# TensorE's matmuls in two stages of a streaming encoder layer: order of tracing released

## The chip, the core and the metric

The kernel runs on one core of a Trainium2 chip. The metric is the device time of one execution in microseconds (us). PE is TensorE's matmul side, PEld its weight loads, DVE VectorE, ACT ScalarE, POOL GpSimd, SP the engine that issues most DMAs. "Granted clock" is the share of full speed that TensorE's clock had: 1.00 is 2.4 GHz, 0.50 is 1.2 GHz.

## The reference

One inference step of one layer: 512 prompt tokens and 32 decode tokens (544 columns in all), width 1024, everything fp32.

```
h = rmsnorm(x); u = h @ w_in            # [q k v | r k v + three low-rank inputs | two gates]
A = differential attention (8 heads, two softmax maps, chunk mask; decode tokens see 512 cached rows)
B = RWKV-7 recurrence (16 heads of 64; per-token state update S = S*w + sa*(kk*a) + v*k, y = S r)
x = x + (sigmoid(g_A) * (A @ w_o_da) + sigmoid(g_B) * (B @ w_o_rw)) @ w_out
x = x + (silu(c1) * c2) @ w_down        # c = causal conv of rmsnorm(x) @ w_up
y = rmsnorm(x)
```

## The kernel before

All activations lie transposed, 128 rows of features by 544 columns of tokens. A large product with a weight matrix ("dense work") goes one block of 128 output rows at a time. `dense_g` takes two PSUM banks from the pool `psd` (3 banks), one for each half of the 544 columns, and runs 48 matmuls of 128x272 over eight slices of the contraction: each weight is split into a high and a low part (`wh`, `wl`), each activation too, and three of the four products are kept. `load_w` fetches a weight tile of four slices by DMA, ACT writes `wh` (L218), DVE or POOL writes `wl` (L219); the pool holds four such pairs, so about 96 matmuls' worth. When the block is done, ACT or DVE takes the result out of the two banks, and only then are they free.

Stage 1 (about 74 to 650 us of the profile) is the recurrence with the dense work of the input projection beside it. It has these strands, each a Python generator:

- `elementwise`: for each of 8 pairs of heads `rw_rates` and `rw_elem`: low-rank products (tiles `lwh`, `lwl`) and sums over a head (`bonesr`), each a group of two matmuls into a bank of the pool `misc` (2 banks), with DVE and ACT work between. They need the projections r, k, v of their pair (tiles `r`, `kr` with two buffers, `vv` with one).
- `recurrence`: for each half of the heads (4 pairs) `rw_super` (products `misc<-arL,bkL`, an inverse computed on DVE with 32x32 transposes at L635, L675, L680, two joining steps) and `rw_chain`: 8 chunks, each a loop of `psq<-S,arL` and `psq<-uv,mt`, a DVE copy `qs`, `psq<-qs,XT`, copies `uv` by DVE and ACT, `psq<-uv,bkt`, the state `S` on DVE, and outputs into `psy`. Each chunk also transposes the next keys and values (`misc<-cst,bkL`, `misc<-cst,vC`), which ACT copies to `bkt` (2 buffers) and `uv` (3 buffers).
- `rw_sample` (decode tokens), `norms` (group norm of the chains' output) and `rotary`.

Stage 2 (about 650 to 913 us) is attention by heads and blocks of 128 queries: `sc<-xK,xQ` scores, softmax on DVE and ACT, `tp<-cst,pd` transposes, `po<-vtok,pdt` weighted values, and per head a normalization whose result `on` (L1122) frees the bank `po`. The dense work that stage 1 left over, and then `w_orw`, run beside it. Stage 3 (from 913 us on) is dense work alone: `w_oda` (reading `dh`, `dl`, which attention writes head by head), `w_out`, `w_up`, `w_down`.

What sets PE's order: the class `Flow` runs the strands against a clock of its own (`PE.now`, the sum of estimated matmul times). A strand that waits says until when (`yield PE.now + 0.9`); until then `Flow` takes steps of the dense work, three matmuls each. This is the order of tracing. While `PE.pinned` is true, each matmul is tied behind the one traced before it, so PE's list is exactly that order. Where it is false, a scheduler puts the list together before the kernel runs: among the matmuls whose inputs and buffers it estimates to be ready, it takes the one traced first. The lists of DVE, ACT, POOL and of the DMA queues are made by it in both kernels. On the chip each engine goes through its list in order and waits where an input isn't there.

`PE.pinned` is set at L493, ahead of stage 1, and cleared after stage 2, so that stage 3 and the start are free already.

Of the kernel before, what the change touches and what calls it, by code (L numbers as in the profile page):

```python
# [161 lines left out]
def tile_hybrid_layer(  # L162
# [26 lines left out]
    PE = Issue(tc, nc.tensor)  # L189
# [300 lines left out]
                            in1=N[:, :, i, 0:i].unsqueeze(2).to_broadcast([128, 2, i, i]), op=ALU.mult)  # L490
            V.tensor_reduce(out=X[:, :, 0:i, i], in_=tv, axis=AX.X, op=ALU.add)

    PE.pinned = True  # L493
    el_free = [0.0]

    def el_group():
# [1146 lines left out]
def _build(nc, shapes):  # L1643
    import concourse.tile as _tile

    args = {n: nc.dram_tensor(n, s, F32, kind="ExternalInput").ap() for n, s in shapes.items()}
    for n, s in _OUTS:
        args[n] = nc.dram_tensor(n, s, F32, kind="ExternalOutput").ap()
    with _tile.TileContext(nc) as tc:
        tile_hybrid_layer(tc, **args)  # L1650
# [11 lines left out]
```

## Time and profile before

| | |
|---|---|
| median of 3 runs | 1418.26 us (1416.24 to 1420.54) |
| time of the profiled execution | 1418.41 us |
| its span | 1416.6 us (1.8 us lie around it) |
| mean granted clock | 0.938 |
| PE busy, share of the span | 1246.9 us, 88% |
| DVE, ACT, POOL busy | 886.1, 587.0, 226.9 us |

Busy times are sums over stages with different limits: in stage 3 PE is busy nearly throughout, in stages 1 and 2 it is not. Matmuls are pipelined: a 128x272 matmul lasts 0.29 us, but the next starts 0.125 us after it. In rows of the timeline the bracket at the end holds the idle time of the engine ahead of the instruction and what ended it.

### The profile page before, as it was taken

What the parts mean: (1) busy time and instruction counts of PE and PEld (TensorE: products, weight loads), DVE (VectorE), ACT (ScalarE), POOL (GpSimd) and SP (SyncE); (2) the same over time, 40 slices, a digit from 0 to 9 for tenths busy, and PEclk for the clock granted to TensorE, in tenths of its full rate; (3) what the DMA queues carried; (4) which work ended last, traced back from release to release, by engine and by line L of the source; (5) the groups of instructions that cost most, each with busy time, mean ns of one, the idle gap of its engine ahead of it and who ended that gap; (6) DMA issues with size and microseconds to landing.
All of it is one profiled execution on the core that took longest, in us unless ns stands there. A gap on an engine that the chain in (4) does not pass through costs nothing.

```text
span 1416.6 us, 29784 instructions
## 1 busy us (share of the span) xinstructions
PE 1246.9 (88%) x12014; PEld 1191.7 (84%) x12014; DVE 886.1 (63%) x1835; ACT 587.0 (41%) x1184; POOL 226.9 (16%) x264
## 2 busy tenths in 40 slices
PE   7789994799879899995998885599999999999997
PEld 6778884788858799885988775499999999999996
DVE  6857659654579333862566676466787878774333
ACT  6655552464312233323564354234544444443220
POOL 6601111111113101224102100000111111111111
PEclk9999998799989899997999997699999999999998
DMA  5254564234667254436553440145322222234321
GB/s 167 77 176 145 175 189 129 75 109 136 183 198 224 72 153 126 156 102 200 167 175 112 127 117 17 48 146 189 110 88 89 89 85 89 90 94 154 104 81 63
DMA packets 135465, 178.01 MB, mean 126 GB/s; under 512 B 41248, under 2 KB 64416, under 8 KB 135328
## 3 DMA queue, kind: packets, MB, share of 16 engines
q1 hardware_dynamic: 122256, 154.86, 35.8%
q10 hardware_dynamic: 13072, 21.26, 4.6%
q8 instruction: 94, 1.54, 0.4%
q14 instruction: 43, 0.35, 0.1%
HBM read 138.39 MB, written 37.41 MB: 124 GB/s over the span
## 4 chain that ended last, share of the span: by engine, by line
PE 69%; DVE 18%; ACT 5%; issue 4%; DMA 2%; POOL 1%; SPq 0%; ACTq 0%; DVEq 0%; POOLq 0%
PE psd L88 54%; PE misc L88 4%; PE psq L88 3%; PE po L88 2%; PE sc L88 2%; PE tp L92 2%; PE psy L88 1%; PE misc L92 1%; DVE NP L675 1%; DVE XT L680 1%; DMA wr<-w_in 1%; DVE mt L626 1%; DVE itmp L489 1%; ACT E L1299 1%; DVE sl L252 1%
## 5 line engine op out<-in xcount | busy, mean ns | idle before, releaser
L218 ACT CAST wh<-wr 128x512 fp32r<-128x512 f32 (+1 forms) x316 | 193.6, 615 | 386.8 <-PE psd L88 331.9
L88 PE MATMUL psd<-h_h,wh 128*128 128x272 f32 x976 | 300.4, 308 | 0.0
L88 PE MATMUL psd<-h_h,wl 128*128 128x272 f32 x976 | 288.9, 296 | 2.0 <-POOL wl L219 2.0
L88 PE MATMUL psd<-h_l,wh 128*128 128x272 f32 x976 | 289.0, 296 | 0.3 <-DVE h_l L443 0.3
L219 DVE TENSOR_TENSOR wl<-wr,wh 128x512 fp32r<-128x512 f32 x230 | 159.0, 694 | 122.3 <-ACT wh L218 116.6
L88 PE MATMUL psd<-xgh,wl 128*128 128x272 f32 x704 | 203.9, 290 | 0.0
L88 PE MATMUL psd<-xgl,wh 128*128 128x272 f32 x704 | 203.3, 289 | 0.0
L88 PE MATMUL psd<-xgh,wh 128*128 128x272 f32 x704 | 202.1, 287 | 0.0
L88 PEld LDWEIGHTS psd<-h_h,wh 128*128 128x128 f32 x976 | 191.8, 197 | 4.6 <-issue 1.4
L88 PEld LDWEIGHTS psd<-h_l,wh 128*128 128x128 f32 x976 | 192.2, 197 | 2.0 <-issue 1.4
L88 PEld LDWEIGHTS psd<-h_h,wl 128*128 128x128 f32 x976 | 191.6, 196 | 2.2 <-POOL wl L219 2.2
L219 POOL TENSOR_TENSOR wl<-wr,wh 128x512 fp32r<-128x512 f32 x86 | 118.0, 1376 | 451.3 <-ACT wh L218 423.6
L88 PEld LDWEIGHTS psd<-xgl,wh 128*128 128x128 f32 x704 | 132.6, 188 | 0.0
L88 PEld LDWEIGHTS psd<-xgh,wl 128*128 128x128 f32 x704 | 132.4, 188 | 0.0
L88 PEld LDWEIGHTS psd<-xgh,wh 128*128 128x128 f32 x704 | 132.1, 188 | 0.1
L88 PE MATMUL psd<-ah,wh 128*128 128x272 f32 x352 | 101.7, 289 | 0.0
L88 PE MATMUL psd<-ah,wl 128*128 128x272 f32 x352 | 101.5, 288 | 0.0
L88 PE MATMUL psd<-al,wh 128*128 128x272 f32 x352 | 101.4, 288 | 0.0
L88 PE MATMUL psd<-mh,wh 128*128 128x272 f32 x256 | 76.3, 298 | 0.0
L88 PE MATMUL psd<-ml,wh 128*128 128x272 f32 x256 | 74.5, 291 | 0.0
L88 PE MATMUL psd<-mh,wl 128*128 128x272 f32 x256 | 74.3, 290 | 0.0
L1460 POOL COPY cvo<-uf 128x2 f32<-128x2 f32 x88 | 36.9, 451 | 220.6 <-DVE uf L1457 220.6
(365 smaller groups left out, 2569.8 us busy)
## 6 DMA issues: line engine op xcount, KB each, us to landing
wr<-w_in SPq DMA_DIRECT2D x132, 256.0 KB, 3.1
wr<-w_up SPq DMA_DIRECT2D x88, 256.0 KB, 2.8
wr<-w_down SPq DMA_DIRECT2D x40, 256.0 KB, 2.7
bkL<-bk_d SPq DMA_DIRECT2D x16, 512.0 KB, 4.9
ar_d<-ar SPq DMA_DIRECT2D x8, 544.0 KB, 2.9
t_d<-qt ACTq DMA_DIRECT2D x16, 272.0 KB, 2.6
rQ<-q_d SPq DMA_DIRECT2D x32, 136.0 KB, 3.6
rK<-k_d SPq DMA_DIRECT2D x32, 136.0 KB, 2.8
```

Source lines behind the costliest of these rows:

```text
L88: ins = self.pe.matmul(out, lhsT, rhs, **kw)
L92: ins = self.pe.transpose(out, in_, ident)
L218: A.copy(out=wh[:, :n], in_=raw)
L219: le.tensor_tensor(out=wl[:, :n], in0=raw, in1=wh[:, :n].bitcast(F32), op=ALU.subtract)
L252: V.tensor_tensor(out=l, in0=x, in1=h.bitcast(F32), op=ALU.subtract)
L489: V.tensor_tensor(out=tv, in0=X[:, :, 0:i, 0:i], in1=N[:, :, i, 0:i].unsqueeze(2).to_broadcast([128, 2, i, i]), op=ALU.mult)
L626: V.tensor_tensor(out=dst[:, h, m0 + 4 * q:m0 + 4 * q + 4, :], in0=pm[h].rearrange("p (m k) -> p m k", m=4), in1=mask.unsqueeze(1).to_broa ...
L675: V.transpose(out=npf[r0:r0 + 32, 0:1024], in_=mt[r0:r0 + 32, h, :, 32 * b:32 * b + 32].rearrange("p m t -> p t m"))
L680: V.transpose(out=XT[r0:r0 + 32, :, 32 * b:32 * b + 32].rearrange("p m i -> p i m"), in_=Xp[r0:r0 + 32].rearrange("p a i -> p i a"))
L1299: A.activation(out=E[:, m, 0:nk], in_=sc[m][:, 0:nk], func=AF.Exp, bias=nm[:, m:m + 1], scale=1.0, accum_out=Z[:, m:m + 1])
L1460: G.tensor_copy(out=cvo[:, t, :, w], in_=u[:, 512 + w::32])
```

## The change

One line: the flag ahead of stage 1 is false, so PE's matmuls of stages 1 and 2 are no longer tied to the order of tracing. The tracing itself, with its steps and estimated times, stays as it is; so do all instructions.

```diff
@@ -490,7 +490,7 @@
             V.tensor_reduce(out=X[:, :, 0:i, i], in_=tv, axis=AX.X, op=ALU.add)
 
-    PE.pinned = True
+    PE.pinned = False
     el_free = [0.0]
```

What the flag does, in `Issue._add`:

```python
        if self.pinned:
            self.tc.keep_in_program_order(ins)
```

## Rows read from the trace of the kernel before

**Rows 1.** Busy time of each engine by stretch: us, busy (count), then granted clock, DMA share, GB/s.
```profile
0.00:74.00 74.00, 57.93 (x391) 53.76 (x392) 56.18 (x75) 45.48 (x82) 44.70 (x49) 0.95 0.38 123
74.00:290.00 216.00, 172.14 (x1868) 164.28 (x1867) 148.18 (x252) 101.03 (x195) 27.34 (x28) 0.91 0.48 146
290.00:488.00 198.00, 168.90 (x2545) 154.29 (x2545) 126.79 (x236) 68.62 (x133) 34.61 (x32) 0.92 0.53 157
488.00:652.00 164.00, 159.23 (x1920) 149.32 (x1920) 81.37 (x180) 56.03 (x116) 28.49 (x24) 0.99 0.44 136
652.00:687.00 35.00, 19.48 (x123) 17.64 (x122) 13.68 (x35) 17.23 (x42) 14.67 (x12) 0.76 0.73 217
687.00:842.00 155.00, 137.78 (x1058) 130.39 (x1057) 98.91 (x304) 79.27 (x226) 20.64 (x15) 0.94 0.45 136
842.00:913.00 71.00, 38.80 (x230) 31.15 (x230) 36.62 (x140) 26.84 (x89) 0.00 (x0) 0.67 0.14 43
913.00:1416.60 503.60, 492.67 (x3889) 490.88 (x3889) 324.42 (x617) 192.50 (x306) 56.45 (x106) 0.99 0.33 104
```

**Rows 2.** What PE waited for, 74 to 488 us: sum, times, longest.
```profile
PE misc L88 <- ACT ssx L251: 17.2, 6, 8.0
PE misc L88 <- DVE lwl L252: 12.6, 1, 12.6
PE misc L92 <- DVE gst L847: 6.5, 1, 6.5
```

**Rows 3.** Timeline of PE, the longest wait of stage 1 and the matmul behind it.
```profile
252.05 0.60 PE L88 MATMUL misc<-lwx,lwl 128*128 128x272 f32 x1 [12.59 <-DVE lwl L252]
252.44 0.43 PE L88 MATMUL psd<-h_h,wh 128*128 128x272 f32 x1
```

**Rows 4.** Timeline of DVE in the same stretch.
```profile
243.90 7.64 DVE L680 STREAM_TRANSPOSE XT<-Xp 32x1024 f32<-32x1024 f32 x4
251.57 0.43 DVE L252 TENSOR_TENSOR lwl<-ss,lwh 128x256 fp32r<-128x256 f32 x1
```

**Rows 5.** Timeline of PE, free matmuls of `w_oda` among attention's, heads 4 to 7.
```profile
827.61 0.28 PE L88 MATMUL psd<-dh,wh 128*128 128x272 f32 x1
...
832.01 0.28 PE L88 MATMUL psd<-dh,wl 128*128 128x272 f32 x1
833.75 0.46 PE L88 MATMUL po<-vtok,pdt 128*128 128x128 f32 x2 [1.46 <-DVE on L1122]
...
853.61 0.77 PE L88 MATMUL po<-vtok,pdt 128*128 128x128 f32 x2 [5.12 <-DVE on L1122]
...
875.92 0.77 PE L88 MATMUL po<-vtok,pdt 128*128 128x128 f32 x2 [4.65 <-DVE on L1122]
...
899.15 0.59 PE L88 MATMUL psd<-dh,wh 128*128 128x272 f32 x1
...
913.82 0.60 PE L88 MATMUL psd<-dh,wh 128*128 128x272 f32 x1 [0.46 <-ACT dh L1141]
```

**Rows 6.** Timeline of PE, one chunk of the second chain.
```profile
498.19 0.29 PE L88 MATMUL psd<-h_l,wh 128*128 128x272 f32 x1
498.31 0.29 PE L88 MATMUL psd<-h_h,wl 128*128 128x272 f32 x1
...
499.06 0.29 PE L88 MATMUL psd<-h_h,wl 128*128 128x272 f32 x1
499.28 0.68 PE L88 MATMUL psq<-qs,XT 64*64 64x64 f32 x16
...
507.33 0.51 PE L88 MATMUL psq<-qs,XT 64*64 64x64 f32 x10
```

**Rows 7.** Timeline of DVE, the copy that the chunk's `psq<-qs,XT` reads.
```profile
497.68 0.42 DVE L793 COPY qs<-psq 128x256 f32<-128x256 f32 x1 [0.30 <-PE psq L88]
```

**Rows 8.** Matmuls into `misc`, 290 to 390 us: duration min/median/max, first to last start.
```profile
L92 PE MATMUL misc<-cst,vC x36: 270/273/329, 300.5 to 365.7; 128*128 128x128 f32 x36
...
L88 PE MATMUL misc<-sl,bonesr x8: 285/289/593, 304.2 to 374.6; 128*128 128x272 f32 x8
...
L88 PE MATMUL misc<-lwx,lwh x4: 292/392/393, 294.5 to 334.1; 128*128 128x272 f32 x4
...
L88 PE MATMUL misc<-lax,lwh x4: 287/332/373, 298.1 to 339.5; 128*128 128x272 f32 x4
```

**Rows 9.** Timeline of PE, waits where no dense work stood ahead of a reader.
```profile
351.92 0.39 PE L88 MATMUL misc<-sl,bonesr 128*128 128x272 f32 x1 [0.37 <-DVE sl L252]
...
862.78 1.65 PE L88 MATMUL po<-vtok,pdt 128*128 128x128 f32 x6 [0.62 <-ACT pdt L1320]
```

**Rows 10.** DMA issues: engine, operation, count, KB each, median us to landing.
```profile
bkL<-bk_d SPq DMA_DIRECT2D x16, 512.0 KB, 4.9
rQ<-q_d SPq DMA_DIRECT2D x32, 136.0 KB, 3.6
```

## The prediction

> **What bounds the kernel now.** I began with the busy times by stretch [rows 1]. From 913 us on PE is busy 492.67 of 503.60 us at a granted clock of 0.99, and those matmuls are free in both kernels: nothing can be won or lost there but what attention leaves behind. The change can act between 74 and 913 us. PE's idle time there is what a passed wait could give back: 216 - 172.14 = 43.9 us up to 290, 29.1 up to 488, only 4.8 up to 652, 15.5 at the change of stages, 17.2 up to 842, and 32.2 in the last 71 us of attention, 142.7 us in all. The granted clock says the same: 0.91 and 0.92 in the first two stretches, 0.99 where PE is full, 0.67 at the end of attention.
>
> Then the waits [rows 2]. The longest is one of 12.59 us, for the low half of a low-rank weight [rows 3]. DVE wrote it at 251.57, right behind four 32x32 transposes that took 7.64 us [rows 4]. In all that time PE did nothing, and as soon as the wait ended it ran dense matmuls whose weights had been there. So a list that let the dense work pass would have had something to do. This is the case for the change.
>
> The case against it I took from a place where this same kernel is free already. `w_oda` is traced after the flag is cleared, and its matmuls may pass attention's [rows 5]. From 827.61 to 832.01 the list holds 36 of them in one run, ahead of a weighted-values group that waits for `on`. That wait is then 1.46 us long; the same wait of the next two heads, without such work, is 5.12 and 4.65 us. So the scheduler sees a wait of this kind and fills it. But 36 is three banks of 12: two halves of the first block and one of the second, each with the four contraction slices whose heads were done. From then on all three `psd` banks belonged to unfinished blocks, and the later waits got only the few matmuls that each new head allowed, some of them at 899.15, until the last head at 913.82. Passing takes whatever is ready and holds the banks until the late input comes. There nobody else wanted `psd` for 80 us. In stage 1 others do.
>
> **The change, part by part.** No instruction is added or removed. What moves is PE's order, and with it the times at which weight buffers, banks and tiles come free for the other engines. Four effects, each with both ends.
>
> *Waits filled (a gain).* A passed wait takes at most what the banks hold, 36 matmuls or 4.7 us by [rows 5]. The idle time of 74 to 488 us is 73.0 us [rows 1], in waits of which the longest three make 8.0, 12.6 and 6.5 us [rows 2]. But dense work done earlier is only worth something where PE was the bound later on. In the chains it partly was. `qs` was written at 497.68 + 0.42 = 498.10 [rows 7], and its reader came at 499.28 because nine dense matmuls stood before it [rows 6]: 1.2 us too late. A chunk has three such hand-overs; I give them 2 us together, so 16 us for the eight chunks of the second chain, and 8 for the first, whose stretch has idle time already. At the change of stages PE idles 15.5 us, but a head without dense work still takes 875.92 - 853.61 = 22.3 us [rows 5], so I credit 2 us. The clock comes back too: a mean of 0.91 over 216 us and 0.92 over 198 us is 38.9 + 31.7 = 70.6 us at half speed [rows 1]. If half of it goes, and a quarter of that time is won (PE is not busy in all of it, and not all that it does then is on the path), that is 9 us. Together 16 + 8 + 2 + 9 = 35 us. Below, nothing; above, all of 73.0 + 15.5 = 88.5 us.
>
> The Trainium skill ("TensorE: Matmul & The Clock Gate", Terms) prices the throttled time at its length times the share of the clock that is missing, here half. For the 35.3 us that I let go it would give 17.6 us instead of 9, and the sum below would be 9 us lower; no run here shows which is nearer.
>
> *Banks held (a loss).* Where the first chain runs, its transposes of coming keys and values and the elementwise strand of the pairs after it share the two `misc` banks [rows 8]. Tied to the trace, a chunk's transposes come when their buffers are about to be free. Released, they are ready as soon as their DMA has landed, pass the late chain step, fill a bank, and then ACT's copy has to wait until the chain frees `bkt` or `uv`. Meanwhile the elementwise groups find no bank. In that stretch there are 8 + 4 + 4 groups of that strand, 16. If each waits half a chunk step, (507.33 - 499.28) / 2 = 4.0 us [rows 6], that is 64 us on the strand that has to end before the second half of the recurrence can start. The lower end is 0, since a freed bank goes to the group traced first. I take 25 us: nearer the lower end, because [rows 5] show that banks do get held, but not that anyone waited.
>
> The Trainium skill ("Trainium Kernel Development and Optimization", Best Practices) says that regular bubbles can mean PSUM has run out. That speaks for this term; what shows it here is only the 80 us in [rows 5] for which `psd` was full.
>
> *Hand-overs without cover (a loss).* Once dense work has been drawn forward, a reader goes into the list right where the scheduler thinks its input is ready. What the chip takes longer than the estimate, PE waits. The rows where a reader stood right behind its writer show 0.37 and 0.62 us [rows 9]. There are 16 chunks with 3 hand-overs and 32 attention blocks with 2, so 112; at 0.5 us that is 56 us, at 0 nothing. Many already have none to spare, and many will keep theirs; I take 20 us.
>
> *Changes of shape (a loss).* The first matmul after another kind comes 0.22 us after its neighbour (499.06 to 499.28) where dense ones follow at 0.12 (498.19 to 498.31) [rows 6], so about 0.1 us for each change and 0.2 for a run of dense work put in between. The chains now have three runs of nine per chunk, 48. A free list fills in ones, twos and fours; at a third of the length there are 96 runs more, 17 to 20 us. None is possible, if the runs stay whole. I take 15 us.
>
> The sum: -35 + 25 + 20 + 15 = +25 us on the span of 1416.6 us, and 1.8 us around it: 1443.4, so 1443 us. The profiled execution (1418.41 us) is within 0.2 us of the median of the runs, so this is also +25 us on 1418.26.
>
> **The rivals.**
>
> *Faster: the waits are filled and nobody misses the banks.* For it speaks the fill at 827.61, which was right to about a microsecond [rows 5], and the ready work behind the 12.59 us wait [rows 3]. Against it, that half of the idle time lies where dense work is no help (the last 71 us of attention) or where the chain's own latency decides. With the gain at 60 us and the losses at 17, the span is 1373.6 and the time 1375 us. It decides from the point where the losses together stay under the gain, in my sum under 35 us of the 60 that I charged.
>
> *Much slower: transfers.* A released group goes into the list when its load is estimated to have landed. The chunk loads of the recurrence and the head loads of attention come from DRAM that was just written; they land in 4.9 and 3.6 us [rows 10]. If the list expects them one such latency too early for the 8 pairs and the 8 heads, that is 8 x 4.9 + 8 x 3.6 = 68 us. With the other terms at zero: 1416.6 + 68 + 1.8 = 1486 us. Against it: the list of `w_oda` missed by little.
>
> *No change: little is passed.* If the scheduler estimates the waiting groups to be ready in time, it puts them where the trace has them, and the time stays at 1418 us. [rows 5] speak against it.
>
> **How the numbers follow.** The forecast of +25 us gets 0.47, the faster rival 0.30, the much slower one 0.15, no change 0.08. A measurement of this kernel tells about 0.3% (4 us) from no change; by that bound slower is 0.47 + 0.15 = 0.62, faster 0.30, same 0.08. The forecast alone would reach from 1424 to 1465 us. The range has to take in most of the faster case and most of the transfers: 1378 to 1490 us.
>
> **What would show it.** Right: the stretch to 488 us has less idle time before the first chain begins, but the step from one `psq<-qs,XT` to the next grows in the first chain; waits for `misc` or `psd` to be put away by ACT appear on PE; the second chain starts later than 499 us; dense runs inside chunks get shorter than nine; the granted clock between 488 and 652 us drops below 0.99. Wrong, to the fast side: the second chain starts well before 490 us, and attention ends before 900. Wrong by transfers: PE waits that end in a DMA, at `arL`, `bkL`, `rQ` or `rK`. No change: the same order of groups on PE.

## The result: 3.2% faster, and where the time went

The changed kernel takes 1372.93 us (median, 1372.07 to 1373.42), against 1418.49 for the kernel before on the same chip. The ratio is 0.9679, with a 95% interval of 0.9662 to 0.9695. I had forecast 1443 us and a range down to 1378, so the time lies below the range, 2 us under that of the rival "Faster" (1375).

The busy times of the changed kernel's trace by stretch, as in [rows 1]:

```profile
0.00:74.00 74.00, 57.92 (x391) 53.95 (x392) 56.11 (x75) 45.57 (x82) 44.55 (x49) 0.95 0.37 123
74.00:290.00 216.00, 197.59 (x2059) 188.40 (x2059) 151.86 (x255) 106.67 (x203) 28.14 (x29) 0.88 0.50 149
290.00:488.00 198.00, 186.75 (x2578) 167.92 (x2578) 126.75 (x243) 70.14 (x140) 39.49 (x33) 0.93 0.57 169
488.00:652.00 164.00, 155.75 (x1819) 145.97 (x1815) 81.25 (x177) 58.22 (x120) 37.87 (x30) 0.99 0.49 151
652.00:687.00 35.00, 30.55 (x191) 26.91 (x190) 27.31 (x77) 22.76 (x64) 7.07 (x5) 0.81 0.61 180
687.00:842.00 155.00, 136.86 (x1006) 121.80 (x1005) 108.84 (x351) 83.97 (x247) 16.24 (x12) 0.92 0.40 119
842.00:913.00 71.00, 58.04 (x441) 54.87 (x440) 37.11 (x104) 22.91 (x55) 0.00 (x0) 0.80 0.33 99
913.00:1371.00 458.00, 447.63 (x3552) 446.25 (x3550) 295.67 (x555) 177.07 (x275) 56.20 (x106) 0.99 0.33 102
```

PE's idle time between 74 and 913 us is 73.5 us, where it was 142.7. Up to 488 us it fell from 73.0 to 29.7, at the change of stages from 15.5 to 4.5. The last stretches of attention don't compare: it now ends at 867, inside the stretch from 842 to 913, and the rest of that stretch is stage 3. Events that both traces have put the gain in its place. The first `psq<-qs,XT` of the second chain starts at 479.65 instead of 499.28, 19.6 us earlier. Attention's first `tp` starts at 634.53 instead of 658.71, 24.2 earlier. The last `tp<-cst,on`, that of the decode tokens, starts at 867.35 instead of 912.92, 45.6 earlier, and from there to the end of the span it is 503.7 us before and 503.8 after. So there are two gains of about the same size: 24 us ahead of attention and 21 in attention, whose length falls from 254.2 to 232.8 us. Attention by itself, before and after:

```profile
658.71:912.92 254.21, 194.91 (x1400) 178.22 (x1400) 149.16 (x476) 121.32 (x351) 29.67 (x22) 0.84 0.39 119
634.53:867.35 232.82, 193.92 (x1377) 171.46 (x1378) 149.55 (x476) 121.80 (x351) 31.35 (x23) 0.87 0.44 132
```

PE's idle time there fell from 59.3 to 38.9 us, by nearly as much as the length.

What PE waited for from 74 to 488 us, as in [rows 2]: sum, times, longest.

```profile
PE misc L88 <- issue: 8.6, 5, 2.6
PE misc L88 <- DVE mt L626: 7.1, 5, 1.7
...
PE misc L88 <- DVE lwl L252: 2.5, 2, 2.1
...
PE misc L92 <- DVE gst L847: 1.8, 1, 1.8
...
PE misc L88 <- ACT ssx L251: 0.4, 1, 0.4
```

The three long waits of [rows 2] are short: `ssx` fell from 17.2 to 0.4 us, `lwl` from 12.6 to 2.5, `gst` from 6.5 to 1.8. The longest wait for `ssx`, before and after:

```profile
227.15 0.59 PE L88 MATMUL misc<-ssx,bonesr 128*128 128x272 f32 x1 [7.96 <-ACT ssx L251]
```

```profile
227.86 0.52 PE L88 MATMUL misc<-ssx,bonesr 128*128 128x272 f32 x2 [0.36 <-ACT ssx L251]
```

The reader starts at nearly the same time, but in the 8 us ahead of 227.15 the list now holds 62 dense matmuls: this wait was filled. `lwl` went another way. First PE's reader, then DVE's part, as in [rows 3, 4]:

```profile
241.17 0.52 PE L88 MATMUL misc<-lwx,lwl 128*128 128x272 f32 x2 [2.08 <-DVE lwl L252]
```

```profile
239.63 1.48 DVE L252 TENSOR_TENSOR lwl<-ss,lwh 128x256 fp32r<-128x256 f32 x1
...
246.01 8.20 DVE L680 STREAM_TRANSPOSE XT<-Xp 32x1024 f32<-32x1024 f32 x4
```

Dense work did not pass this wait; the wait itself went. DVE now writes `lwl` ahead of the transposes behind which it stood before. The lists of all engines are planned together, so releasing PE's list changed DVE's too: at 547 of the 1,835 places in its list another instruction now stands.

One chunk of the second chain, as in [rows 6, 7], first PE, then DVE:

```profile
478.35 0.37 PE L88 MATMUL psd<-h_h,wh 128*128 128x272 f32 x1
...
479.65 0.68 PE L88 MATMUL psq<-qs,XT 64*64 64x64 f32 x16
...
487.70 0.51 PE L88 MATMUL psq<-qs,XT 64*64 64x64 f32 x10
```

```profile
478.05 0.42 DVE L793 COPY qs<-psq 128x256 f32<-128x256 f32 x1 [0.89 <-PE psq L88]
```

`qs` is written at 478.47 and read at 479.65: the reader is 1.2 us late, as before, behind a run of dense matmuls that starts at 478.35. The eight chunks take the same time to 0.02 us: 58.35 from first to last before, 58.37 after.

Attention, heads 4 to 7 and the sample, for [rows 5, 9]. PE's timeline:

```profile
802.88 0.60 PE L92 MATMUL tp<-cst,on 128*128 128x128 f32 x4
...
819.23 1.06 PE L92 MATMUL tp<-cst,on 128*128 128x128 f32 x4
...
832.75 3.94 PE L88 MATMUL sc<-kc,qks 64*32 64x512 f32 x10 [0.25 <-ACT E L1299]
...
837.20 1.06 PE L92 MATMUL tp<-cst,on 128*128 128x128 f32 x4
...
851.83 1.09 PE L92 MATMUL tp<-cst,on 128*128 128x128 f32 x4 [5.01 <-DVE on L1122]
...
867.35 0.45 PE L92 MATMUL tp<-cst,on 128*128 128x128 f32 x1 [4.01 <-DVE on L1122]
```

The heads from 802.88 to 851.83 take 16.4, 18.0 and 14.6 us, where the same ones took 20.1, 22.3 and 18.8. The decode tokens' scores (`sc<-kc,qks`) run at 832.75 ahead of the last head's end (851.83); before, they ran at 897.1, behind it. So groups of other heads and of the sample now run in the waits; whether the gain is theirs or that of dense work, the experiments show. Over the whole trace `po` waits 3.3 us for `on` instead of 18.9.

The DMAs of [rows 10] land as they did (4.9 and 3.6 us before):

```profile
bkL<-bk_d SPq DMA_DIRECT2D x16, 512.0 KB, 5.0
rQ<-q_d SPq DMA_DIRECT2D x32, 136.0 KB, 3.8
```

### The profile page after: what moved, and what is told of

The parts are those of the page before. It is cut to its first block, busy times and chain, and to the rows that moved or that the text cites. A ratio compares the mean times of both kernels' runs of the same rounds, so it can differ in the third digit from the quotient of the medians.

```text
span 1371.1 us, 29786 instructions
## 1 busy us (share of the span) xinstructions
PE 1271.1 (93%) x12014; PEld 1206.1 (88%) x12014; DVE 884.9 (65%) x1835; ACT 587.3 (43%) x1184; POOL 229.6 (17%) x264
## 4 chain that ended last, share of the span: by engine, by line
PE 75%; DVE 14%; ACT 4%; issue 3%; DMA 2%; POOL 1%; SPq 0%; DVEq 0%; ACTq 0%; POOLq 0%
PE psd L88 59%; PE misc L88 5%; PE psq L88 3%; PE psy L88 2%; PE po L88 2%; PE sc L88 2%; PE tp L92 1%; PE misc L92 1%; DVE XT L680 1%; DVE itmp L489 1%; DMA q_d<-qt 1%; DVE NP L635 1%; DVE Xp L491 1%; DMA zr<-z_d 1%; DVE att L269 0%
## 5 line engine op out<-in xcount | busy, mean ns | idle before, releaser
L88 PE MATMUL psd<-h_h,wl 128*128 128x272 f32 x976 | 292.7, 301 | 2.8 <-POOL wl L219 2.6
L88 PE MATMUL psd<-h_l,wh 128*128 128x272 f32 x976 | 293.3, 301 | 0.2 <-DVE h_l L443 0.2
```

What stands on the lines that cost most here:

```text
L88: ins = self.pe.matmul(out, lhsT, rhs, **kw)
```

## The experiments

Each was compared with the kernel before, run on the same chip. A gain in us below is (1 - ratio) x 1418.5; the changed kernel's is 45.5. "Second chain", "start" and "length" of attention are the events above, from each run's trace. Each is read from one execution, and they vary. Five kernels have the changed kernel's order in stage 1; in their traces the second chain starts at 476.1 to 487.3 and attention at 630.9 to 643.6. So attention is compared by its length, which varies less: 251.5 to 254.5 us in four traces with PE tied there, 230.0 to 235.4 in four with it free.

### Which stage: one free at a time

```diff
     proj_dense.finish()
+    PE.pinned = False
```

> Stage 1 stays tied to the order of tracing, only attention (stage 2) is released. Theory A (both stages give, each its own part): the second chain starts at 499 us as before, the stage change at about 658, and attention alone gains what it gained beyond the lead it got from stage 1, about 21 of the 45 us: 1397 us. Theory B (the gain is dense work drawn forward in stage 1; attention is shorter only because less of it is left): 1412 to 1418 us.

For the other run the flag is false ahead of stage 1, and set at this place.

> Only stage 1 is released, attention is tied. Theory A: the second chain starts at about 480 us, attention begins 24 us earlier than before and then keeps its old length: 1394 us. Theory B: attention is shorter too, as in the changed kernel: 1373 to 1378 us.

Stage 2 alone free: ratio 0.983 (0.9803 to 0.9858), 24.1 us; attention 235.4 us long. Stage 1 alone free: 0.9822 (0.9793 to 0.9851), 25.2 us; second chain at 476.1, attention 254.5 us long. The two add up to 49.3 us, about the whole gain. Each stage gives its own half, and attention's half needs no lead from stage 1.

### Which groups: dense work or the others

Two orders instead of one. Dense matmuls are tied among themselves, all others among themselves; either order may pass the other:

```diff
-            self.tc.keep_in_program_order(ins)
+            prev = self.last.get(self.dense)
+            if prev is not None:
+                self.behind(ins, prev)
+            self.last[self.dense] = ins.ins.name
```

> Two orders in stages 1 and 2: the dense matmuls keep their order among themselves, all other groups theirs, but either may pass the other. Theory A1 (dense work that fills waits is the whole gain): 1373 us. Theory A2 (in attention it is groups that pass other groups, as the decode tokens' scores pass the last head): stage 1 keeps its 24 us, attention loses most of its 21 us: 1390 to 1394 us.

The counterpart: a dense matmul is tied behind everything traced before it, so it can't be drawn forward; the other groups may pass one another and dense work.

```diff
-            self.tc.keep_in_program_order(ins)
+            if self.dense:
+                for prev in self.since:
+                    self.behind(ins, prev)
+                self.since = []
+            self.since.append(ins.ins.name)
```

> A dense matmul stays behind everything traced before it, all other groups may pass each other and dense work. Theory A1: nothing is left, 1418 us. Theory A2: stage 1 stays as before, attention gains up to 20 us: 1396 to 1404 us.

Dense free: 0.9771 (0.9738 to 0.9803), 32.5 us. Second chain at 480.7, so all of stage 1's gain; but attention is 249.2 us long, 5.0 of the 21.4 us, and 2.3 under the shortest of the tied traces. Groups free: 0.9826 (0.9792 to 0.9861), 24.7 us. Attention is 232.4 us long, all of its gain. The second chain starts at 489.9, which would be half of stage 1's gain; but this is the trace of the fastest run (1387.38, the median is 1394.65), and by the times the kernel gains no more than with attention alone free (24.1). So stage 1 gains mainly by dense work and other groups passing each other, attention by groups that pass groups. That all this is PE's own order is not shown: each of these kernels has another list on DVE and ACT too, and for attention no run keeps those lists as they were.

### The bank term by itself

The changed kernel, with the transposes of a window's keys and values tied at their place of tracing (the same around both loops):

```diff
+            PE.pinned = True
 ...
+            PE.pinned = False
```

> The kernel after, but the transposes of a window's keys and values (the ones whose early start my prediction charged with +25 us, 0 to 64, because they hold the two misc banks) keep their place behind everything traced before them and ahead of everything traced after them. Theory 'banks held, but hidden under the gains': the term exists, so tying them gives it back and the time falls below the changed kernel's 1373 us, to 1348 to 1366. Rival 'banks never short': in the changed kernel's trace a misc bank is mostly held 0.69 us from the transpose's start to the end of the copy that frees it, and nothing waits for one, so nothing is given back: 1371 to 1376 if the transposes fill no wait themselves, and up to 1385 if each tie also stops the groups around it from passing one another (a tie here is a barrier for all groups).

0.9677 (0.9652 to 0.9702), 1375.44 us: no difference from the changed kernel's 0.9679. Nothing was given back: the loss that I had put on these transposes isn't seen. The run alone does not rule it out, since each tie is a barrier for all groups, and what that costs could hide it.

### The number of dense banks

`psd` with two banks instead of three, first with the order tied, then free:

```diff
-    psd = [psd_scope[0].enter_context(tc.tile_pool(name="psd", bufs=3, space=PSUM, side="right"))]
+    psd = [psd_scope[0].enter_context(tc.tile_pool(name="psd", bufs=2, space=PSUM, side="right"))]
```

> The kernel before, with two PSUM banks for the dense groups (psd) instead of three; the tie stays. It is the base for the next run. With the order tied, a dense group that is traced ahead of a wait stands in it only as far as a bank is free, and the hand-written order already spreads them; expected 1425 to 1450.

> The changed kernel with two dense banks instead of three. Theory 'banks are the room that free groups move in': a dense group can be drawn into a wait only with a bank of its own, so with two banks most of stage 1's gain (19 of the changed kernel's 45 us, the part that the run with only the dense work free brought) goes, and the step from the tied kernel with two banks to this one is 20 to 32 us. Rival 'room was never short': with three banks no wait for a bank stood in TensorE's idle time, with two the free order meets the same limit as the tied one, and the step stays 40 to 50 us. Third: the free order can go round a short bank where the tied one must stop, and the step grows above 50 us.

Tied 1.0061 (1.0042 to 1.0081), 1429.59 us; free 0.9755 (0.9731 to 0.978), 1386.58. Taking the order free is worth 43.0 us with two banks and 45.5 with three. So the theory that banks are the room for passing fell, and the rival ("room was never short") holds. What the bank is worth, 9 to 11 us in either order, lies in stage 3: from the last `tp<-cst,on` to the end it is 512.5 us in both traces instead of 503.7, while attention is no longer than with three banks (251.5 tied, 230.0 free).

The Trainium skill ("Trainium Kernel Development and Optimization", Best Practices) says that regular bubbles can mean PSUM has run out; I had let that speak for the bank term. For `psd` these runs do not bear it out: with a bank less, stages 1 and 2 lose nothing that the traces show. For the two `misc` banks it stays open. Up to the second chain, the waits of PE that by the profile end when DVE or ACT has emptied a `misc` bank (into `mt`, `ss`, `ta`, `vC` and others) sum to 15.8 us before and 11.3 after. They are there, they did not grow, and no run gives `misc` another bank.

### One instruction of DVE

The kernel before, PE tied, and only `lwh` and `lwl` given an earlier place among the instructions to be planned:

```diff
-        split(lw, lwh, lwl)
+        with tc.high_priority(offset=3000): split(lw, lwh, lwl)
```

PE's list comes out the same, instruction by instruction. In DVE's list `lwl` of two pairs moves, that of the sixth of the eight (which the expectation miscounts as the fourth) ahead of the last `NP` transpose and the four `XT` transposes; in ACT's a few instructions change places.

> The kernel before, TensorE's order tied as it was, and one VectorE instruction placed earlier: the low half of the fourth pair's low-rank weight (lwl) goes ahead of the last of four NP transposes and of the four XT transposes, behind which the tied kernel's list has it (it was written at 251.57 us, behind 7.64 us of transposes, while TensorE waited 12.59 us). In the changed kernel VectorE's list, too, has it ahead of them, at 239.63 us, and the wait is 2.08 us. Theory 'the list of VectorE took the wait away': part of stage 1's gain is no passing on TensorE at all but a better list of another engine; the wait falls by about 8 us, the second chain starts 5 to 9 us earlier, and the time is 1409 to 1415 us against some 1420. Rival 'the chain is the bound there': the transposes' own reader, the joining step, sets the start of the chain, so the wait moves and the time stays at 1417 to 1424.

0.9949 (0.9933 to 0.9966), 7.2 us faster. The wait, on PE and on DVE:

```profile
245.36 0.60 PE L88 MATMUL misc<-lwx,lwl 128*128 128x272 f32 x1 [3.48 <-DVE lwl L252]
```

```profile
244.93 0.38 DVE L252 TENSOR_TENSOR lwl<-ss,lwh 128x256 fp32r<-128x256 f32 x1
...
246.41 8.24 DVE L680 STREAM_TRANSPOSE XT<-Xp 32x1024 f32<-32x1024 f32 x4
```

The wait fell from 12.59 to 3.48, the second chain starts at 493.42, 5.9 us earlier. So about a third of what the free order gains in stage 1 is to be had with PE's order as it was, by one instruction on another engine.

### A better version: attention's chain first

The changed kernel, and in stage 2 every matmul and transpose that is not dense is planned as if it had been traced 1500 places earlier. A ready group of a head then goes ahead of ready dense work.

```diff
+        if self.first and not self.dense:
+            with self.tc.high_priority(offset=1500):
+                ins = self.pe.matmul(out, lhsT, rhs, **kw)
+        else:
+            ins = self.pe.matmul(out, lhsT, rhs, **kw)
```

> The kernel after, with one more instruction to the scheduler: in the attention stage every group that is not dense gets a priority 1500 places earlier than its place of tracing, so a ready chain group goes ahead of ready dense work. Theory 'data, not order, now sets the chain': free of the tie, the scheduler already takes the earliest traced ready group, and the stage's remaining idle time of TensorE (31 us in 687 to 913 us of the changed kernel's trace) is waiting for results of other engines that no order shortens: 1369 to 1376. Rival 'the order left is still not the best': a dense group that is taken while a chain group is about to become ready costs the chain up to one dense group's 0.2 us at each of the stage's some hundred hand-overs, so chain-first gains 5 to 15 us: 1358 to 1368. Third: dense work that is pushed late leaves a dense tail after the chain, 1376 to 1390.

0.9415 (0.9379 to 0.945), 1337.29 us: 83.0 us faster than before, 36 faster than the changed kernel. My own theory of the moment ("data, not order") fell, and its rival had the sign but not the size. Attention by itself, and the transposes of `on` of the last head and of the decode tokens:

```profile
632.37:831.84 199.47, 184.07 (x1375) 162.59 (x1376) 144.61 (x476) 120.53 (x351) 31.97 (x23) 0.97 0.50 154
```

```profile
817.08 0.63 PE L100 MATMUL tp<-cst,on 128*128 128x128 f32 x4 [0.29 <-DVE on L1134]
...
831.84 0.30 PE L100 MATMUL tp<-cst,on 128*128 128x128 f32 x1 [0.36 <-DVE on L1134]
```

Attention is 199.5 us long (632.37 to 831.84). PE idles 15.4 us in it, where it was 38.9 in the changed kernel, and the granted clock is 0.97 where it was 0.87.

To see whether this comes from passing dense work or from heads that pass one another, the same with attention's groups tied to one another, dense work free:

```diff
+        if self.first and not self.dense:
+            if self.prev is not None:
+                self.tc.add_manual_dep(ins.ins, self.prev, ..., reason="order")
+            self.prev = ins.ins.name
```

> The run with chain-first in attention (1337 us, 36 below the changed kernel), but attention's groups that are not dense are tied to one another in their order of tracing; the dense work is free. Theory 'dense work stood in front of the heads': what chain-first brings is that a ready head group no longer waits behind dense groups traced before it, and tying the head groups among themselves costs about what passing one another brought without it: 17 us (attention lasted 249.2 us in the run with only dense free, 232.8 in the changed kernel), so 1350 to 1358. Rival 'the heads overlap': chain-first works by drawing the next head's groups past the present head's waits (each head takes 16 to 20 us in its trace, 16 to 32 in the changed kernel's), so with the order among them tied nearly all of it goes and more: 1370 to 1392. Third: with chain-first the passing is of no use any more: 1335 to 1341.

0.9667 (0.9639 to 0.9695), 1376.48 us: all of the 36 us is gone. Its attention:

```profile
643.59:876.32 232.73, 191.11 (x1378) 172.42 (x1378) 148.91 (x476) 122.10 (x351) 31.12 (x23) 0.89 0.43 132
```

With the run that left only dense work free, this makes a table of attention's length (dense work may be passed by head groups in all four):

| | heads' groups in their order | heads' groups free |
|---|---|---|
| planned by place of tracing | 249.2 us | 232.8 us |
| head groups ahead of dense work | 232.7 us | 199.5 us |

Either freedom alone gives 16.5 us, both 49.7, so 17 us come only from the two together; that is well beyond the 3 to 5 us by which such lengths vary. That a head group which goes ahead at once also lets the next head's groups start into its waits is the likely reason; the runs show the sum, not this detail.

Chain-first in stage 1 as well (`PE.first` set ahead of it):

> As the run with chain-first in attention, but in the first stage too. There my prediction credited the second chain with 16 us, and its step stayed at 8.3 us (58.35 us for seven steps before, 58.37 after). Theory 'data, not order': the step is set by the hand-overs between engines, so it stays at 8.2 to 8.4 us and the time within 4 us of the run with chain-first in attention alone. Rival 'dense groups stand in the chain's way': the step falls, to 7 to 8 us, the first chain's too (63.7 us for its steps in the changed kernel), and the time falls by 5 to 20 us below that run, unless the dense work that is put off then stands uncovered behind the chain, in which case the second chain is shorter and the time is the same or longer.

0.9568 (0.952 to 0.9616), 1358.04 us, 21 us slower than chain-first in attention alone. The chain did get faster. Three chunks of the second chain, and attention's first transpose:

```profile
467.76 0.68 PE L92 MATMUL psq<-qs,XT 64*64 64x64 f32 x16
...
475.24 0.68 PE L92 MATMUL psq<-qs,XT 64*64 64x64 f32 x16
...
481.81 0.68 PE L92 MATMUL psq<-qs,XT 64*64 64x64 f32 x16
...
657.00 0.78 PE L100 MATMUL tp<-cst,vt 128*128 128x128 f32 x4 [2.49 <-DMA vt<-v_d]
```

The chunk's step is 7.2 us on average (467.76 to 517.98 for seven) instead of 8.3, which is the 1.2 us late reader of [rows 6, 7] won back: in these three chunks it comes 0.06 to 0.23 us behind DVE's copy `qs`. But attention starts at 657.00, 24.6 us later than with chain-first in attention alone, with a wait for `vt`, a load of the values that stage 1's dense work writes to DRAM. Between the second chain's start and attention PE runs 853 dense matmuls instead of 724. So the dense work was due, and putting it off cost more than the chain gave.

Last, the early `lwl` of above in the best version:

> Chain-first in attention (the run at 1337 us) with the same instruction of VectorE given an earlier place for every pair. In that kernel waits for lwl are still 7.9 us in three places, the longest 5.4. If the list of VectorE still costs TensorE time there: 1329 to 1335. Rival 'the free order has taken what there was': dense work fills or moves the wait, 1334 to 1341, no difference that can be told.

0.9422 (0.9401 to 0.9443), 1339.02 us: no difference from 1337.29. And none could show: the lists of PE, DVE, ACT and POOL come out instruction by instruction as without the edit, with this `lwl` ahead of the transposes in both. The waits for it (7.1 us in three places, 7.9 without the edit; the longest lies at 60 us, ahead of stage 1) tell only how much two traces of the same lists differ. So this run decides nothing between the two theories.

## Why the prediction was wrong, step by step

The forecast had the sign wrong. Two steps failed: the three losses, which I put at 60 us and of which the runs show some 4, and in the gain the view that only dense work can pass, where the groups of attention pass one another. Of the 70.5 us between 1443.4 and 1372.9, 55.6 lie in the losses and 14.9 in the gain.

**Waits filled (a gain, 35 us).** Too small, and credited in the wrong places. Of its parts, the 8 us for the first chain held: from its first to its last `psq<-qs,XT` it takes 63.7 us instead of 70.7. The 16 us of the second chain did not come at all; the step stayed 8.3 us. I had seen that its reader is 1.2 us late behind dense work, and took it that a free list would put it first. But the scheduler takes what was traced first among the ready, and the dense run was traced first. The run with chain-first in both stages shows that about half of it was there to be had: seven steps take 50.2 us instead of 58.35. The 2 us at the change of stages were 4.6. The 9 us of the clock did not show in this pair of traces: by the stretches' mean clocks, time at half speed up to 488 us went from 70.6 to 51.8 + 27.7 = 79.5 us. But one trace does not tell, as the last section shows. And the waits ahead of the first chain and between the two, for which I gave nothing, brought 5.5 and 7.1 us. My sentence "dense work done earlier is only worth something where PE was the bound later on" failed there, in part because the longest wait was not filled but removed, by a better order on DVE. Nor does a passed wait end at the 36 matmuls that I took as the most: the one for `ssx` took 62. The 36 of [rows 5] were blocks whose inputs were missing.

**What the four effects left out.** What misled me about the gain is the case against the change, drawn from [rows 5]: there I looked only at dense work that passes. I wrote that a head "without dense work still takes 22.3 us" and that the last 71 us of attention are where "dense work is no help". The groups of the heads themselves may pass one another, and the sample's too. That is attention's whole gain, 21.4 us: the run with dense work held back has all of it (232.4 us).

**Banks held (a loss, 25 us).** Not seen. Tying just those transposes gives nothing back (0.9677 against 0.9679). In the changed kernel's trace they do hold a bank longer in some cases: mostly 1.28 us from the first transpose to the end of ACT's copy, as before, but up to 4.39 where it was 2.73 at most (the expectation's 0.69 is too short). Yet PE's waits for a `misc` bank fell, from 15.8 to 11.3 us, and those that ended with a copy of these keys or values are 0.2 us before and 0.4 after. I had written myself that [rows 5] show no one waiting; 0, the lower end, was the value to take.

**Hand-overs without cover (a loss, 20 us).** No run isolates this term. In stage 1 there is no sign of it: PE's waits under 1 us between 74 us and the second chain fell from 13.7 to 6.9 us in sum. Nor in attention: the 5.01 and 4.01 us for `on` above are not new, the same two waits were 5.38 and 4.02 before, and `po` had waited more for `on`. Inside the second chain the dense runs stood where they had been, and went on covering.

**Changes of shape (a loss, 15 us).** The mechanism is there, the size isn't. Up to the second chain dense runs went from 96 to 118, so 22 more and not 96; at my 0.2 us that is 4.4 us, an estimate that no run times by itself.

**The rivals.** "Faster" had the time, and its condition holds: the losses stay small. Its account holds for stage 1 alone, since it too expected nothing of attention's end. "Transfers" did not happen: loads land as before, and no new wait for them grew. "No change" fell with the lists. Both signs that I had named for the fast side came: the second chain started before 490 us, and attention ended before 900.

With the three losses at 0, 0 and 4 us, as these traces have them, and the gain as I had it, my own sum would have been -31 us, or 1388; the other 15 us are 21.4 for groups that pass groups, 12.6 for the waits around the first chain, 2.6 more at the change of stages and 1.0 less in the first chain, less 25 credited in vain to the second chain and the clock; and the 4 us of shapes, which the measured parts hold already.

## What to carry to other kernels

A pinned order costs most where independent strands (heads, a sample) stand behind one another's waits; ask of each wait not only which filler work could pass it, but which groups of the other strands could. Order is two decisions: whether groups may pass, and which ready group goes first; giving the latency-bound strand precedence paid twice as much once its groups were free to pass, and turned into a loss where the filler itself had a due time. And when one engine's list is released, read the other engines' lists again before pricing a wait: the longest one here fell to 2.08 us by an instruction of DVE that changed its place.

## What the runs showed that I had not expected

PE's clock can stay at half speed while PE is busy throughout. In the changed kernel's trace, from 126 us on (columns as in [rows 1]):

```profile
126.00:130.00 4.00, 3.64 (x32) 3.12 (x30) 1.74 (x2) 3.50 (x8) 0.00 (x0) 1.00 0.68 256
130.00:132.00 2.00, 0.56 (x4) 0.31 (x3) 1.17 (x3) 2.00 (x5) 1.41 (x3) 1.00 0.02 4
132.00:134.00 2.00, 1.87 (x9) 1.46 (x8) 1.99 (x5) 1.98 (x4) 0.85 (x2) 0.62 0.00 0
134.00:138.00 4.00, 4.00 (x17) 3.52 (x17) 1.75 (x4) 2.36 (x4) 1.48 (x2) 0.50 0.46 147
138.00:142.00 4.00, 4.00 (x19) 3.78 (x18) 2.05 (x3) 0.06 (x1) 0.85 (x1) 0.50 0.34 119
```

PE was idle for 1.44 us of the two ahead of 132, then busy again, and the clock fell to 0.50 only then, and stayed there until about 143 us. In the kernel before, PE was idle for 1.31 us of four at nearly the same place, and the clock stayed at 1.00:

```profile
136.00:140.00 4.00, 2.69 (x18) 2.35 (x18) 2.87 (x5) 1.94 (x5) 2.33 (x2) 1.00 0.60 197
```

And how much time falls to half speed differs from execution to execution. In the traces of the five kernels with the changed kernel's order in stage 1, it is 58 to 82 us between 74 and 488 us (78.5 in the one above), with nearly the same idle time up to the second chain (30 to 34 us). In four traces with PE tied there, with 63 to 74 us of idle time, it is 71.7 three times and 85.3 once. So this pair of traces, with 43 us less idle time and 7 to 9 us more at half speed, does not show what the order does to the clock in stage 1. In attention the lower idle time and the higher clock did go together: 59.3, 38.9 and 15.4 us idle, with 0.84, 0.87 and 0.97, in the kernel before, the changed one and the one with chain-first.
